# Sums of weight blocks: GpSimd additions replaced by DMAs that add into SBUF, with the seven products re-signed

## The chip, the cores and the metric

The kernel runs on one core of a Trainium2 chip. A core has five engines that each work through their own queue in order: TensorE (PE) multiplies matrices into PSUM, VectorE (DVE) and ScalarE (ACT) work on SBUF and PSUM, GpSimd (POOL) works on SBUF, and SyncE (SP) only issues DMAs. Sixteen DMA engines move data between HBM and SBUF; SP and ACT issue DMAs through hardware queues, GpSimd through a software queue. The engines wait for each other and for DMAs with semaphores. The metric is the device time of one execution in microseconds.

## The reference

The reference is one layer of a decoder trunk with 2048 rows of width 1024. All is float32. What costs time are its matrix products:

```python
u = x * (1.0 + scale[:, None, :]) + shift[:, None, :]
h = u @ w_in[l]
q, k, v, a_gate, p_in, p_gate, m_a, m_p = jnp.split(h, offsets, axis=-1)
a = sliding_window_sink_attention(q, k, v, sinks[l], bias, mask) * jax.nn.silu(a_gate)
a = a @ w_attn_proj[l]
p = jnp.einsum('bsgc,gcd->bsgd', multiscale_causal_pool(p_in), w_pool_mix[l]).reshape(B, S, POOL_WIDTH)
p = (p * pool_scale[l]) * jax.nn.silu(p_gate)
p = p @ w_pool_proj[l]
y = jax.nn.sigmoid(m_a) * a + jax.nn.sigmoid(m_p) * p
y = (y @ w_out[l]) * (1.0 + gate[:, None, :])
x = layer_norm(DEEPNORM_ALPHA * x + y, ln_gain[l], ln_bias[l])
```

`w_in` is 1024 x 6400 (16 query heads of 64, 2 key and value heads, and five widths of 1024), `w_attn_proj`, `w_pool_proj` and `w_out` are 1024 x 1024. The attention has a window of 128 with a sink for each head.

## The kernel before, in words

**Float32 by parts.** TensorE multiplies float32r operands. Each operand is split into a high part (a copy that rounds, on ScalarE, lines 312 and 319) and a low part (operand minus high part, on VectorE, through `low`, line 128). A product of blocks is then three matmuls, high by high, high by low and low by high (`mm3`).

**Seven products instead of eight.** The gates, keys and values, the attention and pool projections and the output projection are computed as 2 x 2 block products with seven block products (Winograd's form of Strassen's scheme). A `Quad` holds two weight rows; each row is 128 x 1024 and is cut in two halves of 128 x 512, so that the blocks are a11, a12 (row 0) and a21, a22 (row 1). The data side has blocks b11, b12, b21, b22, each as four tiles of 128 x 512 with high and low parts, and the sums T1 to T4 of them; these eight are the `sets`. They are made once a phase and are shared by all quads of the phase; for later phases they are written to HBM and loaded back. Before the change, with S1 = a21 + a22, S2 = S1 - a11, S3 = a11 - a21, S4 = a12 - S2 on the side of the weights and T1 = b12 - b11, T2 = b22 - T1, T3 = T2 - b11, T4 = b21 - T2 on the other, the seven are a11 b11, S1 T1, S2 T2, a12 b21, S3 T3, S4 b22 and a22 T4.

**The weight tile W.** W (`Pools.weights`, two buffers) has three places of 128 x 512. `load` (lines 270 to 277) loads a21, a22 (in a tile of its own, A22) and a11 through SP and lets GpSimd add S1 into place 1 (`sum1`, line 280). `first` gives the pair a11 and S1 to the split. `mid` (lines 282 to 286) then makes S2 and S3 in place on GpSimd (lines 284, 285) and loads a12 over a11, by a DMA that GpSimd issues. `second` gives a12 and S2, `late` (line 290) makes S4 over a12, and `third` gives S4 and S3.

**Order of one group.** Quads run in groups of two (one group has one). There are 58 quads: 17 for the gates and the keys and values in each half of the sequence, 4 for the attention projection and 4 for the pool projection in each half, and 8 for the output. In `ring`, `back` runs the second pairs of both quads (products with T2 and B21), then the third pairs (T3 and B22), then a22 (T4), and `front` runs the first pairs of the next group's quads (B11 and T1), so that a group is 14 products of twelve matmuls. Each product ends with a `tick`, at which hooks run: pieces of other work (loads and splits of sets, folding of the pool weights, sums of data blocks) that are placed by the number of the tick; `defer` puts a piece some ticks later. In `third` the next quad's `load` stands right behind the split that reads W last. The split's buffers (`w_set`, four of 128 x 1024) hold two pairs, so that a pair is split while the pair before it is multiplied. Engines keep the program's order within their queue where the code says so (`Ordered`), elsewhere a scheduler orders them.

**Stages.** The head modulates x, makes the first sets and does the sums of the first two quads on VectorE. Then come the gates of half 0, the attention of half 0, the gates of half 1, the attention of half 1 (both attentions also make the first products of the next stage, with `early_hi`, `early_lo` and `fill_one`), and last a stage of five rings: attention and pool projection of each half, and the output with the layer norm. The pool projection writes its sum to `y_d` in HBM, from which the output's quads load their weights' side.

Of the kernel before, what the change touches and what calls it, by code (L numbers as in the profile page):

```python
# [58 lines left out]
def kernel(  # L59
# [154 lines left out]
    def sums_to(ph, store, i, load, work, b12):  # L214

        b = []

        def x(r, c):
            return b[r][:, c * CH : (c + 1) * CH]

        def fetch():
            b.extend((ph.spare(), ph.spare()))
            b.reverse()
            for r in (1, 0):
                load(b[r], r)

        def sub(out, a, c):
            return lambda: pool.tensor_tensor(x(*out), x(*a), x(*c), ALU.subtract)

        todo = [(0, fetch), (3, lambda: work(b[0], 0)), (3.5, lambda: work(b[1], 1))]  # L230
        todo += [(at, sub(*z)) for at, z in (
            (7.5, ((0, 1), (0, 1), (0, 0))),
            (9, ((1, 1), (1, 1), (0, 1))),
            (10.5, ((1, 0), (1, 0), (1, 1))),
            (12, ((0, 0), (1, 1), (0, 0))),
        )]
# [25 lines left out]
    class Quad:  # L262
# [3 lines left out]

        def __init__(self, srcs, consume):
            self.srcs, self.consume = srcs, consume

        def load(self, ph, own, q=nc.sync, e=nc.gpsimd):  # L270
            self.w, self.a22 = ph.weights(), ph.last(own)
            x = self.w
            q.dma_start(x[:, 2, :], self.srcs[1][:, 0:CH])
            q.dma_start(self.a22, self.srcs[1][:, CH:])
            q.dma_start(x[:, 0, :], self.srcs[0][:, 0:CH])
            if e is not None:
                self.sum1(e)

        def sum1(self, e):
            e.tensor_tensor(self.w[:, 1, :], self.w[:, 2, :], self.a22, ALU.add)  # L280

        def mid(self, q=nc.gpsimd, e=nc.gpsimd):
            x = self.w
            e.tensor_tensor(x[:, 1, :], x[:, 1, :], x[:, 0, :], ALU.subtract)  # L284
            e.tensor_tensor(x[:, 2, :], x[:, 0, :], x[:, 2, :], ALU.subtract)  # L285
            q.dma_start(x[:, 0, :], self.srcs[0][:, CH:])

        def late(self, e=nc.gpsimd):
            x = self.w
            e.tensor_tensor(x[:, 0, :], x[:, 0, :], x[:, 1, :], ALU.subtract)  # L290

        def first(self):

            return self.w[:, 0:2]
# [5 lines left out]
        def third(self):  # L300

            return self.w[:, 0:3:2]
# [36 lines left out]
    def front(ph, q, tick):  # L339
        w = pair_split(ph, q.first())  # L340
        q.mid()
        a, b = bank(), bank()
        product(a, w[0], "B11", True)
        tick()
        product(b, w[1], "T1", True)
        tick()
        return a, b, None, None

    def back(ph, grp, opened, nxt, own, tick, b22_first=False):
        st = []  # L350
        for q, (a, b, c, w) in zip(grp, opened):
# [10 lines left out]
            nc.vector.tensor_tensor(u2, c, u2, ALU.add)  # L362
# [38 lines left out]
        for q in nxt[len(st) :]:  # L401
            q.load(ph, own)
        for q, b, c, u2, p5 in st:
# [3 lines left out]
            nc.vector.tensor_tensor(u2, c, u2, ALU.add)  # L407
# [266 lines left out]
    def attention(ph, s, q0, nxt):  # L674
# [67 lines left out]
        def finish(kind, store, m, t, src, gate):  # L742
# [7 lines left out]
            if (half, t) == (0, 1):  # L750
                pool.tensor_tensor(x, x, kept[kind, 0, 0], ALU.subtract)
# [7 lines left out]
            pool.tensor_tensor(t1, x, t1, ALU.subtract)  # L759
# [3 lines left out]
            pool.tensor_tensor(b11, t1, b11, ALU.subtract)  # L763
# [53 lines left out]

        def early_hi(x, which):
            hi, lo = ph.split(), ph.split()
            pre[x, which] = hi, lo  # L820
            act.copy(by_two(hi), nxt_group[x].first())

        def early_lo(x, which):
            hi, lo = pre[x, which]
            low(dve, by_two(lo), nxt_group[x].first(), by_two(hi))
# [3 lines left out]
        def pair(x, which):  # L829
            return halves(*pre[x, which])  # L830
# [12 lines left out]
        for n in range(N + 5):  # L843
# [221 lines left out]
    def head(ph):  # L1065
# [57 lines left out]

        def parts(name, i, src):
# [6 lines left out]
        def middle(k):  # L1131

            b1, b2 = xs[k]
            if k < 4:
                t = ts[k] = ph.p("t")
                minus(t, b2, b1)
                pool.dma_start(b12_d[k // 2, :, k % 2, :], b2)
            else:
                minus(ts[k - 4], b2, ts[k - 4])
# [5 lines left out]
        def rest_sums(i):  # L1145
            minus(xs[i][0], ts[i], xs[i][0])
# [6 lines left out]
        def products(i):  # L1153
            for w, (a, b, _, _) in zip(starts, opened):
                product(a, w[0], "B11", True, i, i + 1)
                product(b, w[1], "T1", True, i, i + 1)

        for k in range(KT):
            load(k)
            if k < 2:  # L1160
                grp[k].load(ph, False, sp, None)
# [5 lines left out]
        for k in range(2, KT):  # L1167
# [3 lines left out]
            if k == 2:  # L1171
                for q in grp:
                    q.sum1(dve)
# [15 lines left out]
        for q in grp:  # L1189
            q.late(dve)  # L1190
# [197 lines left out]
```

## Time and profile before

| what | value |
|---|---|
| time, median of 3 runs (lowest to highest) | 1850.66 us (1850.57 to 1857.23) |
| profiled execution: its time / the span of its trace | 1849.77 us / 1848.0 us |
| busy: PE / DVE / ACT / POOL | 1732.7 / 1312.4 / 942.6 / 928.6 us |
| moved by DMA | 381.32 MB, mean 206 GB/s |
| HBM read / written | 244.35 / 138.44 MB |
| granted TensorE clock, mean | 0.98 |

Busy is the time in which an engine executes; issuing a DMA, waiting on a semaphore and branches do not count. A row of a group reads: line, engine, operation, output and inputs by the program's names, count, then busy time in us and the mean of one in ns, then the engine's idle time just before the group and what ended most of it. A row of the waits reads: engine and what it was about to do, what it waited for, total us, how many times, the longest. A row of a timeline starts with the start and the length in us and has the idle time before it in brackets. L55 is the line of a helper that records many operations, so there the tile's name tells which one it is; L128 is the helper of the low parts.

### The profile page before, as it was taken

To read this page: it belongs to the slowest core of one execution; us is meant where nothing else is said; L and a number is where in the kernel's file an instruction comes from. 1 tells how busy PE (TensorE), PEld (TensorE's weight loads), DVE (VectorE), ACT (ScalarE), POOL (GpSimd) and SP (SyncE) were. 2 spreads that over 40 slices of the span, in tenths; PEclk is the share of its full clock that TensorE was granted. 3 is DMA by queue.
4 is the path that set the end of the run, shared out by engine and by line. 5 is a ranking of instruction groups with operands and counts; after the bars stand their busy time and mean duration, and the time that the engine had idled before them with its cause. 6 is when DMAs were issued, how large, how long until landed. Compare 5 with 4: busy or idle time off the path is not lost. (4 is left out here: it accounts for less than half of the span.)

```text
span 1848.0 us, 25300 instructions
## 1 busy us (share of the span) xinstructions
PE 1732.7 (94%) x8248; PEld 1437.6 (78%) x8248; DVE 1312.4 (71%) x2284; ACT 942.6 (51%) x1977; POOL 928.6 (50%) x758
## 2 busy tenths in 40 slices
PE   6789899999999999999999999999989989999996
PEld 6667677788888887787777888888867778777775
DVE  6955656554777777777766457777857887886886
ACT  4533334443777776543444367777724343422453
POOL 2234445451354667445445224456754785476553
PEclk9889999999999999999999999999999999999998
DMA  9245556677254457785776733543876574589432
GB/s 354 97 167 177 205 199 230 233 234 196 93 170 143 153 170 295 264 283 204 261 255 248 253 118 125 177 160 121 301 280 216 174 259 171 200 296 384 147 141 102
DMA packets 163571, 381.32 MB, mean 206 GB/s; under 512 B 19680, under 2 KB 23792, under 8 KB 163440
## 3 DMA queue, kind: packets, MB, share of 16 engines
q1 hardware_dynamic: 150528, 342.95, 53.3%
q0 software_dynamic: 10112, 33.06, 5.2%
q10 hardware_dynamic: 2800, 3.70, 0.9%
q8 instruction: 65, 1.06, 0.2%
q14 instruction: 66, 0.54, 0.1%
HBM read 244.35 MB, written 138.44 MB: 207 GB/s over the span
## 5 line engine op out<-in xcount | busy, mean ns | idle before, releaser
L55 PE MATMUL mm<-set_B,w_set 128*128 128x512 f32 x3240 | 809.6, 398 | 33.7 <-DVE w_set L128 23.3
L55 PEld LDWEIGHTS mm<-set_B,w_set 128*128 128x128 f32 x3240 | 606.8, 191 | 169.5 <-DVE w_set L128 32.4
L55 PE MATMUL lg<-set_T,w_set 128*128 128x512 f32 x2088 | 523.0, 400 | 49.5 <-ACT w_set L312 18.2
L55 PEld LDWEIGHTS lg<-set_T,w_set 128*128 128x128 f32 x2088 | 395.7, 192 | 152.6 <-DVE w_set L128 29.5
L128 DVE TENSOR_TENSOR w_set<-W,w_set 128x1024 fp32r<-128x1024 f32 x162 | 241.2, 1489 | 142.5 <-ACT w_set L312 137.4
L312 ACT CAST w_set<-W 128x1024 fp32r<-128x1024 f32 x162 | 169.5, 1050 | 234.6 <-PE mm L55 159.8
L55 PE MATMUL mm<-set_T,w_set 128*128 128x512 f32 x1080 | 267.1, 395 | 0.0
L55 PEld LDWEIGHTS mm<-set_T,w_set 128*128 128x128 f32 x1080 | 202.4, 190 | 42.2 <-DVE nxt L55 0.2
L284 POOL TENSOR_TENSOR W<-W 128x512 f32<-128x512 f32 x56 | 85.2, 1522 | 148.3 <-DVE w_set L128 129.0
L290 POOL TENSOR_TENSOR W<-W 128x512 f32<-128x512 f32 x56 | 80.1, 1430 | 157.8 <-DVE w_set L128 146.4
L363 POOL TENSOR_TENSOR p<-p,u 128x512 f32<-128x512 f32 x58 | 98.0, 1693 | 93.6 <-DVE u L362 91.4
L280 POOL TENSOR_TENSOR W<-W,A 128x512 f32<-128x512 f32 x56 | 82.5, 1473 | 109.1 <-DMA A<-in_win_dram 46.4
L55 DVE TENSOR_TENSOR o<-pv,o 64x128 f32<-64x128 f32 x256 | 72.4, 283 | 90.0 <-ACT o L55 87.1
L55 ACT ACTIVATE L<-L,nm 128x257 f32<-128x257 f32 (+1 forms) x256 | 127.8, 501 | 8.5 <-DVE nm L55 3.2
L55 DVE TENSOR_TENSOR k_lo<-spare,k_hi 128x512 fp32r<-128x512 f32 x88 | 89.7, 1027 | 48.4 <-ACT k_hi L55 24.4
L55 DVE CUSTOM_DVE_ANT_0 L<-lg,bt,nsink 128x256 f32<-128x256 f32 (+1 forms) x256 | 111.6, 473 | 5.3 <-PE lg L55 1.2
L285 POOL TENSOR_TENSOR W<-W 128x512 f32<-128x512 f32 x56 | 90.0, 1610 | 12.1 <-DMA W<-in_win_dram 9.5
L55 POOL TENSOR_TENSOR w_set<-W,w_set 128x1024 fp32r<-128x1024 f32 x14 | 33.7, 2408 | 122.8 <-ACT w_set L55 54.7
L55 POOL TENSOR_TENSOR p<-nxt,pg 128x512 f32<-128x512 f32 x32 | 41.4, 1294 | 105.1 <-DVE sm L55 103.8
L55 ACT COPY o<-pv 64x256 f32<-64x256 f32 x128 | 47.4, 371 | 80.8 <-PE pv L55 78.6
L55 DVE TENSOR_TENSOR ptl<-pt,pth 128x512 fp32r<-128x512 f32 (+1 forms) x128 | 85.8, 670 | 1.8 <-ACT pth L55 1.6
L55 ACT CAST k_hi<-spare 128x512 fp32r<-128x512 f32 x88 | 53.6, 616 | 55.2 <-POOL spare L55 20.3
(201 smaller groups left out, 2520.1 us busy)
## 6 DMA issues: line engine op xcount, KB each, us to landing
W<-in_win_dram SPq DMA_DIRECT2D x68, 256.0 KB, 3.8
w_set<-wmix_d SPq DMA_DIRECT2D x32, 512.0 KB, 5.4
A<-in_win_dram SPq DMA_DIRECT2D x34, 256.0 KB, 3.8
W<-in_win_dram POOLq DMA_DIRECT2D x34, 256.0 KB, 3.8
ag_d<-sig SPq DMA_DIRECT2D x32, 256.0 KB, 3.0
pg_d<-sig SPq DMA_DIRECT2D x32, 256.0 KB, 3.1
ma_d<-sig SPq DMA_DIRECT2D x32, 256.0 KB, 3.5
mp_d<-sig SPq DMA_DIRECT2D x32, 256.0 KB, 3.4
```

Of the source, the lines that this page charges most:

```text
L55: return lambda *args, **kw: self.tc.keep_in_program_order(op(*args, **kw))
L128: engine.tensor_tensor(dst, src, as32(hi), ALU.subtract)
L280: e.tensor_tensor(self.w[:, 1, :], self.w[:, 2, :], self.a22, ALU.add)
L284: e.tensor_tensor(x[:, 1, :], x[:, 1, :], x[:, 0, :], ALU.subtract)
L285: e.tensor_tensor(x[:, 2, :], x[:, 0, :], x[:, 2, :], ALU.subtract)
L290: e.tensor_tensor(x[:, 0, :], x[:, 0, :], x[:, 1, :], ALU.subtract)
L312: a.copy(by_two(hi), raw)
L363: nc.gpsimd.tensor_tensor(p5, p5, u2, ALU.add)
```

## The change

The four sums of weight blocks that GpSimd made in SBUF for each quad become DMAs issued by GpSimd with `accum_op=ALU.add`: each reads a block of the weights from HBM and adds it to what lies in its place of W. Since such a DMA only adds, the seven products are written with plus signs on the side of the weights: S1 = a21 + a22, S2' = S1 + a11, S3' = a11 + a21, S4' = S2' + a12, and on the other side T1 = b11 - b12, T2 = b22 + T1, T3 = b11 - T2, T4 = b21 - T2. The products with T1 and T2 keep their pairing, and where a product now has the other sign, the addition behind it on VectorE is a subtraction.

In W, place 0 now holds a12, place 1 the running sum and place 2 a11 and then S3'. So a12 has a place of its own and is loaded with the other blocks by SP. S1 is asked for two ticks behind the loads (`defer(2, q.sum1)`), in the attentions at step 53 where the loads are at step 51. `mid` issues two adding DMAs behind the split of the first pair, `late` one behind the split of the second. For 56 quads that is four adding DMAs in place of four GpSimd instructions and one plain DMA; a plain DMA more goes through SP. The first two quads keep their sums on VectorE, with four instructions each as before.

```diff
         def __init__(self, srcs, consume):
             self.srcs, self.consume = srcs, consume
-
-        def load(self, ph, own, q=nc.sync, e=nc.gpsimd):
+            self.a11, self.a12 = srcs[0][:, 0:CH], srcs[0][:, CH:]
+            self.a21 = srcs[1][:, 0:CH]
+
+        def load(self, ph, own, q=nc.sync, a12=True):
             self.w, self.a22 = ph.weights(), ph.last(own)
             x = self.w
-            q.dma_start(x[:, 2, :], self.srcs[1][:, 0:CH])
+            q.dma_start(x[:, 1, :], self.a21)
             q.dma_start(self.a22, self.srcs[1][:, CH:])
-            q.dma_start(x[:, 0, :], self.srcs[0][:, 0:CH])
-            if e is not None:
-                self.sum1(e)
-
-        def sum1(self, e):
-            e.tensor_tensor(self.w[:, 1, :], self.w[:, 2, :], self.a22, ALU.add)
-
-        def mid(self, q=nc.gpsimd, e=nc.gpsimd):
-            x = self.w
-            e.tensor_tensor(x[:, 1, :], x[:, 1, :], x[:, 0, :], ALU.subtract)
-            e.tensor_tensor(x[:, 2, :], x[:, 0, :], x[:, 2, :], ALU.subtract)
-            q.dma_start(x[:, 0, :], self.srcs[0][:, CH:])
-
-        def late(self, e=nc.gpsimd):
-            x = self.w
-            e.tensor_tensor(x[:, 0, :], x[:, 0, :], x[:, 1, :], ALU.subtract)
+            q.dma_start(x[:, 2, :], self.a11)
+            if a12:
+                self.load_a12(q)
+
+        def load_a12(self, q):
+            q.dma_start(self.w[:, 0, :], self.a12)
+
+        def add(self, place, src):
+            nc.gpsimd.dma_start(self.w[:, place, :], src, accum_op=ALU.add)
+
+        def sum1(self):
+            self.add(1, self.srcs[1][:, CH:])
+
+        def mid(self):
+            self.add(1, self.a11)
+            self.add(2, self.a21)
+
+        def late(self):
+            self.add(1, self.a12)
 
         def first(self):
-            return self.w[:, 0:2]
+            return self.w[:, 1:3]
 
         def second(self):
             return self.w[:, 0:2]
 
         def third(self):
-            return self.w[:, 0:3:2]
+            return self.w[:, 1:3]
...
-            nc.vector.tensor_tensor(u2, c, u2, ALU.add)
+            nc.vector.tensor_tensor(u2, u2, c, ALU.subtract)
...
+        def ask(q):
+            q.load(ph, own)
+            defer(2, q.sum1)
+
         def third(x):
             w[x] = pair_split(ph, st[x][0].third())
             if x < len(nxt):
-                nxt[x].load(ph, own)
+                ask(nxt[x])
...
-            nc.vector.tensor_tensor(p5, c, p5, ALU.add)
+            nc.vector.tensor_tensor(p5, c, p5, ALU.subtract)
...
-            if n == 51:
-                for q in nxt_group:
+            for q in nxt_group:
+                if n == 51:
                     q.load(ph, False)
+                if n == 53:
+                    q.sum1()
...
             if k in (3, 5):
-                grp[k // 2 - 1].mid(pool, dve)
+                q = grp[k // 2 - 1]
+                q.load_a12(pool)
+                plus(q.w[:, 1, :], q.w[:, 1, :], q.w[:, 2, :])
+                minus(q.w[:, 2, :], q.w[:, 1, :], q.a22)
```

The sums of data blocks (in `sums_to`, `finish` and the head) swap operands or signs in the same places, on the same engines.

More of the change, by code (lines that the diff above doesn't have):

```diff
@@ L225, in fetch, with put_sum @@
                 load(b[r], r)
-        def sub(out, a, c):
-            return lambda: pool.tensor_tensor(x(*out), x(*a), x(*c), ALU.subtract)
+        def put_sum(out, a, c, op):
+            return lambda: pool.tensor_tensor(x(*out), x(*a), x(*c), op)
         todo = [(0, fetch), (3, lambda: work(b[0], 0)), (3.5, lambda: work(b[1], 1))]
[L231 to L235, printed above, removed]
+        todo += [(at, put_sum(*z)) for at, z in (
+            (7.5, ((0, 1), (0, 0), (0, 1), ALU.subtract)),
+            (9, ((1, 1), (1, 1), (0, 1), ALU.add)),
+            (10.5, ((1, 0), (1, 0), (1, 1), ALU.subtract)),
+            (12, ((0, 0), (0, 0), (1, 1), ALU.subtract)),
         )]
@@ L401, in back @@
         for q in nxt[len(st) :]:
-            q.load(ph, own)
+            ask(q)
         for q, b, c, u2, p5 in st:
@@ L816, in attention, with raw_pair @@
         pre = {}
+        def raw_pair(x, which):
+            return nxt_group[x].second() if which else nxt_group[x].first()
         def early_hi(x, which):
@@ L820, in early_hi @@
             pre[x, which] = hi, lo
-            act.copy(by_two(hi), nxt_group[x].first())
+            act.copy(by_two(hi), raw_pair(x, which))
         def early_lo(x, which):
             hi, lo = pre[x, which]
-            low(dve, by_two(lo), nxt_group[x].first(), by_two(hi))
+            low(dve, by_two(lo), raw_pair(x, which), by_two(hi))
             if which:
```

32 lines of the change are left out of this document (17 added, 15 removed).

## The prediction

> **What bounds the kernel now.** I read the page first: the shares of the engines, the slices and the DMA queues.
>
> ```profile
> span 1848.0 us, 25300 instructions
> PE 1732.7 (94%) x8248; PEld 1437.6 (78%) x8248; DVE 1312.4 (71%) x2284; ACT 942.6 (51%) x1977; POOL 928.6 (50%) x758
> ...
> DMA  9245556677254457785776733543876574589432
> GB/s 354 97 167 177 205 199 230 233 234 196 93 170 143 153 170 295 264 283 204 261 255 248 253 118 125 177 160 121 301 280 216 174 259 171 200 296 384 147 141 102
> ...
> q1 hardware_dynamic: 150528, 342.95, 53.3%
> q0 software_dynamic: 10112, 33.06, 5.2%
> ```
>
> TensorE is busy 94% of the span, so the most that any change beside it can win is its idle time, 1848.0 - 1732.7 = 115 us. The view of windows, cut at the stages, tells where that lies (columns: window, its length, then busy time of PE, PEld, DVE, ACT and POOL, granted clock, DMA share, GB/s):
>
> ```profile
> 92.00:450.00 358.00, 330.03 (x1464) 266.80 (x1463) 211.15 (x242) 142.76 (x212) 158.04 (x133) 0.96 0.61 203
> 450.00:730.00 280.00, 277.68 (x1568) 241.99 (x1568) 207.11 (x630) 206.20 (x610) 151.67 (x125) 1.00 0.51 174
> 730.00:1030.00 300.00, 287.58 (x1234) 232.09 (x1233) 212.42 (x226) 138.23 (x211) 148.27 (x109) 0.98 0.71 252
> ...
> 1435.00:1530.00 95.00, 85.75 (x357) 68.23 (x356) 84.65 (x67) 33.93 (x40) 74.41 (x57) 0.96 0.63 216
> ...
> 1600.00:1690.00 90.00, 85.39 (x371) 68.71 (x370) 72.02 (x55) 24.37 (x30) 70.82 (x58) 1.00 0.79 288
> 1690.00:1848.00 158.00, 135.39 (x583) 109.17 (x581) 121.00 (x170) 66.91 (x103) 70.34 (x53) 0.96 0.43 160
> ```
>
> The first attention (450 to 730) leaves 2.3 us. The rings of seven products, which the change touches, leave 28.0 us in the first gates, 12.4 in the second, and 9.3, 4.6 and 22.6 in three parts of the last stage, 77 us in all. In the pool products (1435 to 1530) VectorE is busy 89% and GpSimd 78%. The waits of TensorE say for what:
>
> ```profile
> PE mm L55 <- DVE w_set L128: 23.3, 19, 3.7
> PE lg L55 <- ACT w_set L312: 18.2, 11, 5.1
> PE lg L55 <- DVE w_set L128: 15.9, 19, 5.5
> ...
> PE mm L55 <- ACT w_set L312: 6.3, 3, 2.8
> ```
>
> So 63.7 us is waiting for a weight's split: its high part (ScalarE, L312) or its low part (VectorE, L128). What follows asks what the change does to those two.
>
> **GpSimd's sums go.** Four sums for each of 56 quads (the first two quads sum on VectorE):
>
> ```profile
> L284 POOL TENSOR_TENSOR W<-W 128x512 f32<-128x512 f32 x56 | 85.2, 1522 | 148.3 <-DVE w_set L128 129.0
> L290 POOL TENSOR_TENSOR W<-W 128x512 f32<-128x512 f32 x56 | 80.1, 1430 | 157.8 <-DVE w_set L128 146.4
> L363 POOL TENSOR_TENSOR p<-p,u 128x512 f32<-128x512 f32 x58 | 98.0, 1693 | 93.6 <-DVE u L362 91.4
> L280 POOL TENSOR_TENSOR W<-W,A 128x512 f32<-128x512 f32 x56 | 82.5, 1473 | 109.1 <-DMA A<-in_win_dram 46.4
> ...
> L285 POOL TENSOR_TENSOR W<-W 128x512 f32<-128x512 f32 x56 | 90.0, 1610 | 12.1 <-DMA W<-in_win_dram 9.5
> ```
>
> and, from the same grouping for GpSimd alone, its next two groups:
>
> ```profile
> L546 POOL TENSOR_TENSOR wide<-gp,wide 128x512 f32<-128x512 f32 x32 | 50.2, 1569 | 7.6 <-DVE gp L544 7.2
> L55 POOL TENSOR_TENSOR spare<-spare 128x512 f32<-128x512 f32 x32 | 47.5, 1485 | 7.1 <-issue 4.9 <-DVE k_lo L55 1.0 <-POOL W L290 0.7
> ```
>
> That is 82.5 + 85.2 + 90.0 + 80.1 = 337.8 us of GpSimd's 928.6. GpSimd bounds nothing, so this in itself is worth 0. But it slows VectorE's splits, which have the same shape always and yet take 1.2 to 5.8 us. The instructions of the tile W (min/median/max ns, first and last start):
>
> ```profile
> L312 ACT CAST w_set<-W x162: 1029/1052/1063, 65.4 to 1817.4; 128x1024 fp32r<-128x1024 f32 x162
> L128 DVE TENSOR_TENSOR w_set<-W,w_set x162: 1205/1226/5762, 72.9 to 1818.5; 128x1024 fp32r<-128x1024 f32 x162
> ...
> L275 SPq DMA_DIRECT2D W<-in_win_dram x32: 422/426/728, 74.6 to 1014.6; - x32
> L286 POOL DMA_DIRECT2D W<-in_win_dram x32: 557/557/574, 94.2 to 1027.5; - x32
> ```
>
> The mean of those 162 is 1489 ns (row below), so they lose (1489 - 1226) x 162 = 43 us to something.
>
> ```profile
> L128 DVE TENSOR_TENSOR w_set<-W,w_set 128x1024 fp32r<-128x1024 f32 x162 | 241.2, 1489 | 142.5 <-ACT w_set L312 137.4
> ```
>
> The longest lies beside GpSimd additions that follow each other without a gap, of which these are two (timeline, VectorE and GpSimd):
>
> ```profile
> 1653.18 5.76 DVE L128 TENSOR_TENSOR w_set<-W,w_set 128x1024 fp32r<-128x1024 f32 x1 [0.23 <-ACT w_set L312]
> ```
>
> ```profile
> 1654.07 1.29 POOL L280 TENSOR_TENSOR W<-W,A 128x512 f32<-128x512 f32 x1
> ...
> 1656.57 1.28 POOL L285 TENSOR_TENSOR W<-W 128x512 f32<-128x512 f32 x1
> ```
>
> In the rings GpSimd's other long work is L363 and the two groups of 50.2 and 47.5, so the removed sums are 337.8 of 533.5 us, 63%. Of TensorE's 39.2 us behind L128 some 6 are the half microsecond that any late high part brings after it; of the other 33, 63% is 21 us as one end, and 0 the other, if VectorE was late through the length of its queue alone. I take two thirds of 21, **-14 us**, since the longest waits lie in the stages where both engines are fullest. A long wait also costs clock: ten matmuls took 4.14 us after a wait of 3.73 us, and 2.56 after 1.57.
>
> ```profile
> 1503.85 4.14 PE L55 MATMUL mm<-set_B,w_set 128*128 128x512 f32 x10 [3.73 <-DVE w_set L128]
> ...
> 1512.73 2.56 PE L55 MATMUL mm<-set_B,w_set 128*128 128x512 f32 x10 [1.57 <-DVE w_set L128]
> ```
>
> Two such fewer are **-3 us** (0 to -9).
>
> **The block a12 is loaded early, by SP.** Before, GpSimd sent for it after L284, because it took the place of a11. ScalarE waited for it and for GpSimd's sums:
>
> ```profile
> ACT sig L517 <- DMA wmix_d<-st_lo: 27.8, 3, 9.8
> ...
> ACT w_set L312 <- DMA W<-in_win_dram: 16.4, 4, 6.0
> ...
> ACT w_set L312 <- POOL W L280: 11.4, 4, 4.0
> ```
>
> Those two are 27.8 us of ScalarE. TensorE's whole waiting for the high part is 18.2 + 6.3 = 24.5 us, and part of it follows other waits in ScalarE's queue, such as the one for a store above them. **-4 us**, ends 0 and -24.5. The 56 more issues on SP, at 0.43 us, are 24 us in a queue that is not the bound; behind them stand stores whose buffers ScalarE reuses, cost 0 unless the queue backs up (counted with the DMA load below).
>
> **Four accumulating DMAs for each quad.** The trace has none, so the cost is bounded. On GpSimd's queue an issue takes 557 to 574 ns (row above): 224 issues less 56 that go to SP, 168 x 0.56 = 94 us, which leaves GpSimd at about 685 us; hidden. The wait that matters is from issue to landing. GpSimd's plain transfers of this size, and all loads into this tile (min/median/max):
>
> ```profile
> DMA to landing us min/median/max: 2.8/3.7/6.3
> ```
>
> ```profile
> DMA to landing us min/median/max: 2.5/3.7/12.9
> ```
>
> So the ends are 2.8 and 12.9 us. I take 5: the median and something for the destination that has to be read too. What it is hidden under: a product of twelve matmuls takes 2.72 us.
>
> ```profile
> 174.81 2.88 PE L55 MATMUL mm<-set_B,w_set 128*128 128x512 f32 x12
> 177.53 2.93 PE L55 MATMUL lg<-set_T,w_set 128*128 128x512 f32 x12
> ```
>
> A group is 14 products, 38 us. The four split buffers let a quad's first, second and third split start four products apart, 10.9 us; less 1.05 + 1.23 = 2.3 us for the split itself, 8.6 us are left for the sum between them. Before, the second split's a12 took 1.5 + 0.56 + 3.7 = 5.8 us of that and the third's sum 1.4. After, both take 0.56 + 5. So 0, with 3 us to spare, and about 112 x each microsecond over it as an upper end; the two quads of a group are late together, so 56 x is what I would count. The first sum is asked for two products after its loads and has about six products; 0. A late one stands in front of GpSimd's L363 add and the later adds of the other quad, as the sums did.
>
> The DMA engines: 33.06 MB took 5.2% of 1848 us, so 256 KB take 0.76 us of all sixteen. 224 more are 170 us, share 59.6 to 69%. Stores and loads that ScalarE and VectorE wait for land later by perhaps 15%; on the 24.5 - 4 us of TensorE's waits for ScalarE that is **+3**. Where the queue is full already, 1600 to 1690 with 0.79, sixteen adds are 12 us of 90 and the next stage's sets and rows come later: **+5** (0 to +15).
>
> The Trainium skill, Collectives: The Full Stack, section The bandwidth ceiling, says that the add in the DMA path costs little in itself but needs two source reads, so that its rate is half a copy's. No run here shows it yet; by that page the 170 us would be 340. The trace's price for a copy is the one that the sum uses.
>
> The Trainium skill, SBUF — State Buffer, section SBUF: two separate sides, warns against moving work to DMAs issued by GpSimd, since a VectorE instruction that holds both ports keeps it from writing descriptors. The 32 issues above lie within 17 ns of each other beside a VectorE that is busy 71%, so the trace does not agree for the instructions of this kernel; by that page each add would be late by up to the length of one VectorE instruction, still under the 3 us spare.
>
> **Signs and order.** The products trade adds for subtractions on the same engines with the same shapes, the places in the weight tile change, and the head does its eight sums on VectorE as before: 0. Only a12 of the head arrives earlier, which nothing waits for.
>
> **Sum.** Against the profiled execution of 1849.8 us (0.9 below the median of 1850.7): -14 - 3 - 4 + 3 + 5 = -13, so 1836.8; on the median's scale **1837 us**.
>
> **Rivals.**
> - Slower: the accumulating DMA lands after more than 8.0 us (8.6 less the issue). Then each second and third split is late, 28 groups x 2 x the excess. At 9 us that is +56, and 1837 + 56 = 1893; at 8.4 it is +22 and 1859. For it: the maximum of 12.9, stages with DMA shares of 0.71 and 0.79. Against: a median of 3.7. It decides from about 8.2 us.
> - No change: each add takes the DMA engines 1.5 us instead of 0.76, for the second read. Then sixteen in the window from 1600 are 24 of 90 us on a share of 0.79, which is full; the rings from 730 get 0.71 + 0.30. I add 6 + 4 us there and 3 more for ScalarE's waits: 1837 + 13 = 1850. Against it: a share of 0.71 at 252 GB/s is not the limit, since another slice moves 384. (The doubled rate is that of the Trainium skill, Collectives: The Full Stack, as above.)
> - Much faster: VectorE's and GpSimd's mutual delay is what all ring waits come from. Half of the 77 us gone is 1850.7 - 38 = 1812. For it: the 89% of VectorE at 1435. Against: 24.5 us of waits are ScalarE's, and the end of the last window is the last rows' own.
>
> **How the numbers follow.** A measurement of this kernel tells about 0.5%, 9.3 us, from no change: 1841.4 to 1859.9. Forecast (1820 to 1841) 0.33, much faster 0.14, no change 0.17, slower 0.36, of which I put 0.14 beyond 1890. The forecast's own range is 1820 to 1848. With 0.05 below 1802 the range 1802 to 1890 leaves out 0.19. Faster 0.47, same 0.17, slower 0.36.
>
> **What the profile after would show.** L128's mean falls from 1489 towards 1300 ns and TensorE's waits for it below 30 us; GpSimd near 685 us; the accumulating DMAs land in 4 to 6 us; no wait of ScalarE's L312 split for a W transfer totals over 20 us. The prediction is wrong if they land in 8 us or more, if ScalarE's waits for W grow past 100 us, or if L128's mean stays while the sums are gone.

## The result and the profile after

The changed kernel takes 1899.99 us (median of 4 runs, 1895.87 to 1904.26), the kernel before beside it 1850.62 us: ratio 1.0268 with the interval 1.0245 to 1.0291, **49 us slower**. The prediction said 1837 and a range up to 1890. The profiled execution has a span of 1902.2 us, 54.2 more than before. From the page after, the shares of the engines, the slices of the DMA share and the queues:

```profile
span 1902.2 us, 25529 instructions
PE 1748.9 (92%) x8248; PEld 1442.0 (76%) x8248; DVE 1226.1 (64%) x2284; ACT 940.1 (49%) x1977; POOL 748.2 (39%) x702
...
DMA  9378798986344579899989833555988898899864
...
q1 hardware_dynamic: 158592, 357.64, 54.0%
q0 software_dynamic: 37888, 77.11, 20.8%
```

VectorE (1312.4 to 1226.1) and GpSimd (928.6 to 748.2) have less work, and still TensorE is idle 153.3 us, 38 more than before, and busy 16 us more with the same matmuls. The software queue grew from 5.2% to 20.8% of the sixteen engines, and outside the attentions the slices of the DMA share are mostly at 8 and 9, where they were at 5 to 7. The same windows as before (columns as there):

```profile
92.00:450.00 358.00, 327.32 (x1453) 263.00 (x1453) 201.83 (x241) 143.11 (x213) 117.36 (x120) 0.97 0.86 243
450.00:730.00 280.00, 278.92 (x1577) 243.16 (x1575) 207.53 (x630) 204.31 (x609) 146.47 (x122) 1.00 0.55 180
730.00:1030.00 300.00, 271.44 (x1121) 217.52 (x1122) 173.96 (x210) 124.84 (x191) 91.47 (x86) 0.95 0.91 274
```

The DMA share in the gates went from 0.61 to 0.86 and from 0.71 to 0.91; in the second gates TensorE does 1121 matmuls in 300 us where it did 1234, and its granted clock falls from 0.98 to 0.95. The attention between them hardly changes. The waits of TensorE, then of ScalarE, for what the change touches:

```profile
PE mm L55 <- DVE w_set L128: 38.1, 28, 4.8
PE lg L55 <- ACT w_set L318: 23.6, 13, 6.7
PE lg L55 <- DVE w_set L128: 16.9, 22, 5.5
PE lg L55 <- DMA set_T<-u_T_split: 9.7, 2, 6.2
PE lg L55 <- DMA set_T<-ain_T_split: 9.1, 3, 6.7
...
PE mm L55 <- ACT w_set L318: 6.1, 3, 4.4
```

```profile
ACT w_set L318 <- DMA W<-y_d: 52.3, 10, 11.0
ACT w_set L318 <- DMA W<-in_win_dram: 45.9, 12, 7.5
ACT w_set L318 <- DMA W<-in_wpp_dram: 16.8, 4, 5.7
ACT w_set L318 <- DMA W<-in_wap_dram: 13.9, 2, 10.2
```

The waits for splits are 84.7 us (63.7 before), and behind them ScalarE waits 128.9 us for transfers into W, in 28 waits. Which transfers these are is told by the view of line 286, which before issued the plain DMA of a12 and now issues the adds. Who waited for it, and for how many us and how often, before and after:

```profile
ACT w_set L312: 37.3, 10
```

```profile
ACT w_set L318: 128.8, 28
```

So all 28 waits end with an adding DMA, none with a plain load. Two groups, and the instructions of lines 128 and 286 (min/median/max ns), the last line being the landing of the adding DMAs of L286 in us:

```profile
L128 DVE TENSOR_TENSOR w_set<-W,w_set 128x1024 fp32r<-128x1024 f32 x162 | 218.1, 1347 | 177.3 <-ACT w_set L318 173.6
...
L286 POOL DMA_DIRECT2D W<-in_win_dram x128 | 112.2, 950 | 408.8 <-DVE w_set L128 238.0
```

```profile
L128 DVE TENSOR_TENSOR w_set<-W,w_set x162: 1207/1225/3705, 73.0 to 1872.8; 128x1024 fp32r<-128x1024 f32 x162
L286 POOL DMA_DIRECT2D W<-in_win_dram x128: 850/874/1219, 77.5 to 1068.1; - x128
```

```profile
DMA to landing us min/median/max: 3.6/6.2/11.5
```

VectorE's splits did become faster (mean 1489 to 1347 ns). An adding DMA takes GpSimd 0.95 us to issue, not 0.56, and lands after 6.2 us; counted from the trace, 31 of the 224 take 8 us or more. They aren't alone in being late: the plain transfers of the same size, before, after, and in the changed kernel with its adds left out (first experiment; count, KB each, median us to landing):

```profile
W<-in_win_dram SPq DMA_DIRECT2D x68, 256.0 KB, 3.8
...
A<-in_win_dram SPq DMA_DIRECT2D x34, 256.0 KB, 3.8
...
ag_d<-sig SPq DMA_DIRECT2D x32, 256.0 KB, 3.0
```

```profile
W<-in_win_dram SPq DMA_DIRECT2D x100, 256.0 KB, 5.4
...
A<-in_win_dram SPq DMA_DIRECT2D x34, 256.0 KB, 6.2
ag_d<-sig SPq DMA_DIRECT2D x32, 256.0 KB, 4.5
```

```profile
W<-in_win_dram SPq DMA_DIRECT2D x100, 256.0 KB, 4.6
...
A<-in_win_dram SPq DMA_DIRECT2D x34, 256.0 KB, 4.7
ag_d<-sig SPq DMA_DIRECT2D x32, 256.0 KB, 4.1
```

So a part of this lateness, 0.8, 0.9 and 1.1 us, is there without any add, in the new form itself (its 100 loads by SP hold a12 besides a21 and a11); the adds bring 0.8, 1.5 and 0.4 us more.

Where the time went by stage shows in the first and last start of the loads into W. The last load of the gates and the loads of the output projection, before, after, and with the adds left out:

```profile
L273 SPq DMA_DIRECT2D W<-in_win_dram x32: 327/333/609, 74.2 to 1014.2; - x32
...
L273 SPq DMA_DIRECT2D W<-y_d x8: 319/327/870, 1649.4 to 1780.3; - x8
```

```profile
L276 SPq DMA_DIRECT2D W<-in_win_dram x32: 327/332/543, 74.3 to 1043.5; - x32
...
L276 SPq DMA_DIRECT2D W<-y_d x8: 319/326/542, 1699.2 to 1835.3; - x8
```

```profile
L276 SPq DMA_DIRECT2D W<-in_win_dram x32: 327/332/688, 73.5 to 980.9; - x32
...
L276 SPq DMA_DIRECT2D W<-y_d x8: 319/327/417, 1606.0 to 1733.8; - x8
```

Against the form without adds, the changed kernel is 63 us behind at the end of the gates, 93 at the start of the output and 102 at its end. Both the gates and the last rings lose.

### The profile page after: what moved, and what is told of

It is laid out like the page before. It is cut to its first block, busy times and chain, and to the rows that moved or that the text cites. A ratio compares the mean times of both kernels' runs of the same rounds, so it can differ in the third digit from the quotient of the medians.

```text
span 1902.2 us, 25529 instructions
## 1 busy us (share of the span) xinstructions
PE 1748.9 (92%) x8248; PEld 1442.0 (76%) x8248; DVE 1226.1 (64%) x2284; ACT 940.1 (49%) x1977; POOL 748.2 (39%) x702
## 3 DMA queue, kind: packets, MB, share of 16 engines
q0 software_dynamic: 37888, 77.11, 20.8%
## 5 line engine op out<-in xcount | busy, mean ns | idle before, releaser
L55 PE MATMUL mm<-set_B,w_set 128*128 128x512 f32 x3240 | 813.4, 399 | 50.9 <-DVE w_set L128 38.1
L55 PE MATMUL lg<-set_T,w_set 128*128 128x512 f32 x2088 | 534.2, 406 | 70.9 <-ACT w_set L318 23.6
L55 PEld LDWEIGHTS lg<-set_T,w_set 128*128 128x128 f32 x2088 | 400.5, 195 | 180.8 <-DVE w_set L128 31.2
L128 DVE TENSOR_TENSOR w_set<-W,w_set 128x1024 fp32r<-128x1024 f32 x162 | 218.1, 1347 | 177.3 <-ACT w_set L318 173.6
L286 POOL DMA_DIRECT2D W<-in_win_dram x128 | 112.2, 950 | 408.8 <-DVE w_set L128 238.0
L369 POOL TENSOR_TENSOR p<-p,u 128x512 f32<-128x512 f32 x58 | 91.7, 1589 | 122.3 <-DVE u L368 113.0
L55 DVE TENSOR_TENSOR k_lo<-spare,k_hi 128x512 fp32r<-128x512 f32 x88 | 74.0, 846 | 95.1 <-ACT k_hi L55 44.3
L55 PE MATMUL lg<-kk,qs 128*128 128x256 f32 (+1 forms) x512 | 80.5, 279 | 0.0
L55 ACT CAST pth<-pt 128x512 fp32r<-128x512 f32 (+1 forms) x128 | 73.5, 574 | 10.6
L55 ACT ACTIVATE L<-L,sm 128x256 f32<-128x256 f32 (+1 forms) x128 | 64.3, 502 | 26.8 <-DVE sm L55 26.7
```

The costliest lines, as they stand in the source:

```text
L55: return lambda *args, **kw: self.tc.keep_in_program_order(op(*args, **kw))
L128: engine.tensor_tensor(dst, src, as32(hi), ALU.subtract)
L286: nc.gpsimd.dma_start(self.w[:, place, :], src, accum_op=ALU.add)
L369: nc.gpsimd.tensor_tensor(p5, p5, u2, ALU.add)
```

## The experiments

Two theories. **Load**: an adding DMA takes the sixteen DMA engines about 1.5 us instead of 0.76, so that all transfers land later. **Chain**: the adds' own issue and landing are too late for the split that waits for them. They don't exclude each other, since by the first the adds land later too. Differences below are the ratio's, times 1850.66 us; the intervals are 3 to 7 us to each side.

**1. No adds.** `add` does nothing.

```diff
-            nc.gpsimd.dma_start(self.w[:, place, :], src, accum_op=ALU.add)
+            pass
```

> The changed kernel with the 224 adding DMAs left out: W holds a12, a21 and a11 as loaded and is split so (the weights' sums are not made, so the output is another one). Two theories on the 49 us. LOAD: each adding DMA takes the sixteen DMA engines some 1.5 us (q0 rose from 5.2% to 20.8%), and every other transfer lands later, on which ScalarE, VectorE and GpSimd wait. CHAIN: the adds themselves land too late for the next split (median 6.2 us behind an issue of 0.95 us, in a gap of 8.6 us), the load on others matters little. Both expect here the change without its price: the gain of 13 to 21 us that was forecast for GpSimd's removed work and the early a12, so about 1830 to 1837 us. If it is above 1845, the gain itself was not there, and the forecast failed on that side too.

1803.4 us, ratio 0.9746 (0.9715 to 0.9776), -47 us. So the adds cost 97 us, and what the change takes away is worth far more than I had put on it (experiments 9 to 11).

**2. Plain DMAs in place of the adding ones.** Same instructions in the same order, without the addition.

```diff
-            nc.gpsimd.dma_start(self.w[:, place, :], src, accum_op=ALU.add)
+            nc.gpsimd.dma_start(self.w[:, place, :], src)
```

> The changed kernel with each adding DMA made a plain one of the same blocks (it overwrites the place, so the sums are not made and the output is another one): the same number of instructions in the same order, the same dependences. LOAD expects each to take about 0.76 us of the DMA engines in place of 1.5, so half of the added load, and a time about half-way between the kernel without adds and the change: 1860 to 1870 us. CHAIN expects a landing of 4 to 5 us, which fits the gap, and so 1832 to 1845 us.

1855.5 us, ratio 1.0015 (0.9995 to 1.0034). The plain copies cost 50 us and the adding 47 more. That is 4.5 us under the range of the load theory and 10.5 over that of the chain theory.

**3. Adds of 64 of the 512 columns.** Every issue and wait stays.

```diff
-            nc.gpsimd.dma_start(self.w[:, place, :], src, accum_op=ALU.add)
+            nc.gpsimd.dma_start(self.w[:, place, 0:64], src[:, 0:64], accum_op=ALU.add)
```

> The changed kernel with each adding DMA cut to 64 of the 512 columns (the sums are made in those columns only, so the output is another one): the same 224 issues with the same dependences and nearly the same order, an eighth of the bytes. Without adds the kernel took 1803.4 us, with plain ones 1855.5, with adding ones 1900. LOAD, by its time on the DMA engines (0.2 us each in place of 1.5): 1803 + 97/8 = 1815 us, 1808 to 1822. CHAIN, in which the issue and the fixed part of the landing count (an issue near 0.9 us and a landing of some 3 us, each in a chain): half of the price or more stays, 1835 to 1860 us.

1822.04 us, ratio 0.9836 (0.9808 to 0.9863): the upper end of what load had expected. An issue still takes 0.95 us on GpSimd, so the issue time costs at most the 17 us that are left. The software queue of the three, each with its span:

```profile
span 1800.8 us, 24928 instructions
...
q0 software_dynamic: 5632, 18.38, 2.8%
```

```profile
span 1856.2 us, 25529 instructions
...
q0 software_dynamic: 23552, 77.11, 12.4%
```

```profile
span 1818.4 us, 25565 instructions
...
q0 software_dynamic: 37888, 25.73, 7.4%
```

Share times span, less the 50.4 us that the queue has without adds (0.028 x 1800.8), over 224: a plain copy takes the sixteen engines (0.124 x 1856.2 - 50.4) / 224 = 0.80 us, an adding one (0.208 x 1902.2 - 50.4) / 224 = 1.54 us, and one of 64 columns 0.38 us.

**4 and 5. One add less.** Without the DMA that makes S3', which has the most time, or without the one that makes S2', which the second split waits for.

```diff
             self.add(1, self.a11)
-            self.add(2, self.a21)
```

> The changed kernel without the add that makes S3' (a11 stays in its place; the output is another one). It stands in no tight place: its result is wanted only by the third split. LOAD: a quarter of the load, so a quarter of the 97 us: 1872 to 1880 us. CHAIN: nearly nothing, 1892 to 1900, since the adds that the splits wait for are all still there.

```diff
-            self.add(1, self.a11)
             self.add(2, self.a21)
```

> The changed kernel without the add that makes S2', for which the second split waits (the place keeps S1; the output is another one). The same engines' order as the kernel without the add of S3', and the same load. LOAD expects the same time as that one, 1872 to 1880 us. CHAIN expects much less, 1835 to 1865, since the second split then waits for nothing that GpSimd issues behind the first split.

1867.64 us (ratio 1.0092, 1.0057 to 1.0128) and 1865.79 us (1.0066, 1.0043 to 1.0089), 4 and 6 us below what load had expected, and equal within their intervals. If a late sum alone were the cause, the hurried one would have been worth more. Against the form without adds, with ScalarE's waits that end with one of these DMAs (who waited for line 286, as above):

| kernel | DMA engines' time for the adds | ScalarE's waits for them | cost over no adds |
|---|---|---|---|
| adds of 64 columns | 84 us | 27.1 us | 17 us |
| plain copies | 180 us | 59.0 us | 50 us |
| no S3' / no S2' | 265 / 271 us | 120.9 / 89.4 us | 64 / 59 us |
| changed kernel | 345 us | 128.8 us | 97 us |

The cost follows the DMA engines' time at 0.2 to 0.28 us for each, whatever makes it: plain, adding, hurried or not. The splits' waits for these DMAs grow with it, so this table doesn't part load from chain. Only the two kernels with one add less speak against the waits as the measure: their load and cost are nearly the same, and their waits differ by 31 us.

**6 and 7. The load on the kernel before.** Behind each of GpSimd's sums goes a DMA that adds the same block into memory that nothing reads; then the same with 64 columns.

```diff
+        def spill(self, src):
+            k = spilled[0] = (spilled[0] + 1) % SCR
+            pool.dma_start(scr[k], src, accum_op=ALU.add)
...
+                self.spill(self.srcs[1][:, CH:])
```

> The kernel before, with the load alone added: behind each of its 224 sums on GpSimd one adding DMA of the same block, into one of four blocks of HBM in turn that nothing reads. Nothing of the products waits for them. LOAD expects a time near or above the change, 1880 to 1910 us, with all landings later as in the change. CHAIN expects 1850 to 1862, what 224 more issues on GpSimd's queue may cost.

1984.26 us, ratio 1.0715 (1.0676 to 1.0754): +132, more than load alone had allowed.

```diff
-            pool.dma_start(scr[k], src, accum_op=ALU.add)
+            pool.dma_start(scr[k][:, 0:64], src[:, 0:64], accum_op=ALU.add)
```

> This is the kernel before with a DMA that adds behind each of GpSimd's sums, as in the loaded kernel before, but each adds 64 of the 512 columns into memory that nothing reads: the output is whole. It keeps the 224 issues on GpSimd's queue (0.95 us each, 213 us in all) and takes seven eighths of the bytes away. If the +134 us of the loaded kernel were transfers on the DMA engines, the time is 1860 to 1885 us: an eighth of the price, and something for sums that start an issue later. If they were the issues in GpSimd's queue, it stays at 1950 to 1985 us.

1912.34 us, ratio 1.0354 (1.032 to 1.0387): +66, between the two expectations. The issues alone cost here, because GpSimd also makes its sums: 128 of the 224 in the view of groups are

```profile
L55 POOL DMA_DIRECT2D scr<-in_win_dram x128 | 115.0, 977 | 1.3 <-issue 1.1
```

an instruction of about a microsecond in front of the next sum. If the small transfers cost the 17 us here that they cost in experiment 3, some 49 of the 66 are issue time in a busy queue, and 132 - 49 = 83 the load of the whole ones. No run tests this division, and experiment 8 shows that a target in memory has a price of its own.

**8. The load without the wait.** The changed form without sums; the 224 adds go to memory that nobody waits for.

```diff
-            nc.gpsimd.dma_start(self.w[:, place, :], src, accum_op=ALU.add)
+            k = spilled[0] = (spilled[0] + 1) % SCR
+            pool.dma_start(scr[k], src, accum_op=ALU.add)
```

> This is the changed kernel with the 224 adds aimed at memory that nothing reads and nobody waits for; the sums of weights are not made, so the product is not the reference's. Issues and bytes stay, the wait of ScalarE and TensorE for the adds is gone. Load theory (each add takes 1.5 us or more of the sixteen DMA engines and every other transfer lands later): 1880 to 1930 us, as the changed kernel. Chain theory (the adds' own landing is what the splits wait for): 1803 to 1830 us, as without any adds.

1971.12 us, ratio 1.0674 (1.0645 to 1.0703). So the load costs without the chain: no split waits for an add, and it is slower still. That doesn't show that the splits' waits for adds cost nothing in the changed kernel, since this run is slower than load had it too and has waits of its own. The adds take the engines 1.6 us each here, and GpSimd waits for earlier ones:

```profile
L55 POOL DMA_DIRECT2D scr<-in_win_dram x128 | 108.5, 1033 | 71.3 <-DMA scr<-in_win_dram 71.3
```

Why a target in memory costs that much more than one in SBUF wasn't settled.

**9. GpSimd's sums in the new form.**

```diff
-            self.add(1, self.a11)
-            self.add(2, self.a21)
+            x = self.w
+            nc.gpsimd.tensor_tensor(x[:, 1, :], x[:, 1, :], x[:, 2, :], ALU.add)
+            nc.gpsimd.tensor_tensor(x[:, 2, :], x[:, 1, :], self.a22, ALU.subtract)
...
```

> The changed kernel's re-signed products, its layout of W and its early a12, but the four sums are made by GpSimd instructions again (S3' as S2' minus a22). The forecast's term for the early a12 was -4 us (0 to -24.5), and signs and order 0: 1846 us, with 1826 to 1851 as ends. LOAD and CHAIN both expect it below the changed kernel by about 50 us, and GpSimd near 920 us busy again. If it is near 1900, the cause is in the layout, the loads through SP or the deferred first sum, and both theories fall.

1863.08 us, ratio 1.0071 (1.0045 to 1.0097), above the ends of the expectation: the new form with the old engine is 13 us slower than the kernel before. So something in the new form beside the adds costs time; experiments 10 and 11 look for it.

**10. The kernel before without GpSimd's sums.** a21 goes to place 1, and the third pair is places 0 and 1.

```diff
-            q.dma_start(x[:, 2, :], self.srcs[1][:, 0:CH])
+            self.whole = e is None
+            q.dma_start(x[:, 2 if self.whole else 1, :], self.srcs[1][:, 0:CH])
...
-            if e is not None:
-                self.sum1(e)
...
+            if self.whole:
+                e.tensor_tensor(x[:, 1, :], x[:, 1, :], x[:, 0, :], ALU.subtract)
...
```

> This is the kernel before without GpSimd's 224 sums of weights: a21 is loaded to the place of the first sum, the products use the blocks as they are, and the block a12 is still sent for by GpSimd once the first split has been made; the product is not the reference's. It is to say what the changed form's 1803 us without adds is owed to. If the sums are what costs in the kernel before (through VectorE's splits and the wait for the sums themselves), it is 1803 to 1815 us. If the early a12 and the new places are worth as much as the sums, it stays at 1825 to 1840 us, as the prediction's first term (14 to 21 us for the sums) would have it.

1792.48 us, ratio 0.9684 (0.9655 to 0.9712): below the expected range. GpSimd's sums hold 58 us, and the old form without sums is 11 us faster than the new one without sums. Its shares and TensorE's first waits:

```profile
span 1784.4 us, 25030 instructions
PE 1706.5 (96%) x8248; PEld 1429.8 (80%) x8248; DVE 1207.6 (68%) x2284; ACT 941.5 (53%) x1977; POOL 591.7 (33%) x534
```

```profile
PE mm L55 <- DVE w_set L128: 10.0, 10, 2.5
PE lg L55 <- DVE w_set L128: 8.8, 8, 5.5
...
PE lg L55 <- ACT w_set L314: 7.6, 6, 3.5
```

The span is 63.6 us shorter than before (this execution ran 6 us under the median of its kernel): 37.4 of it idle time and 26.2 TensorE's busy time, with the mean granted clock at 0.989 instead of 0.980 (0.972 in the changed kernel).

**11. When a12 is loaded.** Both runs are without sums: `add` does nothing, as in experiment 1. First GpSimd sends for it where `mid` stands; then it also goes to the place of a11, so that it has to wait for the first split.

```diff
-        def load(self, ph, own, q=nc.sync, a12=True):
+        def load(self, ph, own, q=nc.sync, a12=False):
...
         def mid(self):
+            self.load_a12(nc.gpsimd)
```

> This is the changed kernel's form without any sums, but the block a12 is sent for by GpSimd at the place in its queue where the sums between the splits stood, as in the kernel before, and not by SP with the other loads; the product is not the reference's. The changed form without sums took 1803 us, the kernel before without sums 1792. If the early load by SP is what makes the changed form slower (four blocks at once in one queue), it is 1788 to 1797 us; if the places in the weight tile or the re-signed products do, it is 1800 to 1806 us.

1805.91 us, ratio 0.9742 (0.9723 to 0.976), as with SP. But GpSimd had nothing to wait for and sent for a12 in the same microseconds as SP for the other blocks, so this told only that the queue doesn't matter.

```diff
-            q.dma_start(self.w[:, 0, :], self.a12)
+            q.dma_start(self.w[:, 2 if self.ring else 0, :], self.a12)
...
-            return self.w[:, 0:2]
+            return self.w[:, 1:3] if self.ring else self.w[:, 0:2]
```

> This is the changed form without sums, with the block a12 loaded by GpSimd into the place of a11, so that it must wait for the first split, as in the kernel before; the order of the instructions on TensorE, ScalarE, GpSimd and SP is that of the kernel before without sums, and VectorE differs by the signs alone; the product is not the reference's. In the run before this one GpSimd sent for a12 in the same 2 us as SP for the other blocks, so it left the four loads together. If four blocks asked for at once are what makes the changed form slower than the one before (1803 against 1792 us without sums), it is 1788 to 1797 us; if the signs or the places are, 1800 to 1808 us.

1795.15 us, ratio 0.9688 (0.9655 to 0.972), that of the old form (0.9684). So four blocks asked for at once cost about 10 us. The same 68 loads that SP makes for W, in the first of these two runs, with a12 beside them, and in the second:

```profile
W<-in_win_dram SPq DMA_DIRECT2D x68, 256.0 KB, 4.6
```

```profile
W<-in_win_dram SPq DMA_DIRECT2D x68, 256.0 KB, 3.9
```

**12. Other engines for the sums.** Half by DMA (S1, S3') and half by GpSimd; all four on VectorE; S2' and S4' on VectorE with S1 and S3' on GpSimd; and the kernel before with S2 and S4 (L284, L290) on VectorE. The last one's edit:

```diff
-            e.tensor_tensor(x[:, 1, :], x[:, 1, :], x[:, 0, :], ALU.subtract)
+            nc.vector.tensor_tensor(x[:, 1, :], x[:, 1, :], x[:, 0, :], ALU.subtract)
...
-            e.tensor_tensor(x[:, 0, :], x[:, 0, :], x[:, 1, :], ALU.subtract)
+            nc.vector.tensor_tensor(x[:, 0, :], x[:, 0, :], x[:, 1, :], ALU.subtract)
```

> The changed kernel with S1 and S3' made by adding DMAs and S2' and S4', for which a split waits soonest, by GpSimd instructions. Both resources have half of the work: 112 adds (LOAD: 48 us over 1803.4) and 112 GpSimd sums (half of what all four cost in the same form, (1863.1 - 1803.4)/2 = 30 us). If the prices add, 1882 us; if a price grows faster than the work, since a half-loaded queue hides more, below 1850, which would beat both kernels. CHAIN expects the second, 1835 to 1850.

> This is the changed kernel's form with all four sums of weights made by VectorE in place of the DMAs, S3' as S2' less a22; the output is whole. No DMA load, and GpSimd has no sum to make. VectorE gets 224 sums of 0.69 us by its own rows of 512 columns, 154 us, and was busy 1226 of 1902 us. Load theory: without the adds the form runs in 1803 us, and what comes on top is only what VectorE's splits come later by; the chain per set is longer by four times 0.69 us on VectorE, so 1815 to 1850 us, at or under the kernel before. Chain theory (any serial sum in the slot is dear): 1850 to 1880 us.

> This is the changed kernel's form with S2' and S4' made by VectorE and S1 and S3' by GpSimd (S3' as S2' less a22); the output is whole. No DMA load; GpSimd's half of the sums is 169 us, VectorE gets 112 of 0.69 us, 77 us. Load theory: 1815 to 1850 us, between the form without sums and that with GpSimd's sums (1863 us). If only GpSimd's slow sums cost, half of the 60 us they cost goes: 1833 us.

> This is the kernel before with the two sums that stand between splits, L284 and L290, made by VectorE (0.7 to 0.9 us each in its earlier runs) instead of GpSimd (1.4 to 1.5 us), and the other two left on GpSimd; the output is whole. If a sum costs by how long the split waits for it and by GpSimd's running beside VectorE's splits, as in the new form with two sums on each, the time is 1825 to 1842 us. If the new form's 1843 us came from the early a12, it is 1845 to 1860 us here.

| sums made by | time | ratio (interval) |
|---|---|---|
| DMA and GpSimd | 1879.94 us | 1.015 (1.0117 to 1.0183) |
| VectorE | 1845.65 us | 0.9986 (0.9971 to 1.0002) |
| VectorE and GpSimd, new form | 1843.03 us | 0.9965 (0.9948 to 0.9982) |
| VectorE and GpSimd, old form | 1842.88 us | 0.9953 (0.9935 to 0.9971) |

The mix costs 75 us over no sums, where half of the DMAs' 97 and half of GpSimd's 60 are 78: the prices add. The last two beat the kernel before by some 6 to 9 us. On whatever engine, the four sums cost 40 to 60 us over the same form without them; the DMAs' 97 is the dearest.

## Why the prediction was wrong

**What was right.** GpSimd's sums did slow VectorE's splits: the mean fell from 1489 to 1347 ns and the longest from 5762 to 3705, and with the sums back on GpSimd in the new form (experiment 9) the mean is 1498. The form without adds is 47 us faster, so there was a gain to be had. Of the three marks that I set for a wrong prediction, one came: ScalarE's waits for W passed 100 us. TensorE's waits for L128 are 38.1 + 16.9 = 55.0 us, not below 30, because its splits now start later.

**The step that failed: the adds at 0, with +3 and +5 for the DMA load.** I took the price of a plain copy, 0.76 us of the sixteen engines, and called a share of 0.61 or 0.71 room enough. An add takes 1.54 us, and the room isn't free: each microsecond of added DMA time cost 0.2 to 0.28 us of the kernel (experiments 1 to 5), long before the share reaches 1. The 345 us cost 97, and even plain copies, 180 us at nearly the price that I had taken, cost 50 and not 8. The sums weren't hidden either. I had 5 us for the landing and 3 to spare; the median is 6.2, and all 28 waits of ScalarE for transfers into W, 128.8 us, end with an add. Only 5 of these 28 adds took 8 us or more, the others landed in 4.0 to 7.9 us: the 8 us that I had allowed were not free. Other transfers land later too, by 0.4 to 1.5 us against the form without adds. Had the add cost what a copy does, the kernel would have been at the time of before (experiment 2).

The Trainium skill, Collectives: The Full Stack, section The bandwidth ceiling, has the add of a ring's reduce step need two source reads and run at half a copy's rate; 1.54 against 0.80 us agrees. The Trainium skill, DMA: Bandwidth & Descriptors, section SWDGE vs HWDGE vs iDMA, says that a DMA engine takes turns between the queues that software and hardware feed. That SP's loads into W land 0.8 us later with the adds in GpSimd's queue than without them (5.4 and 4.6 us) agrees with it; no run here shows the turns themselves.

**The rivals.** "No change" had the right mechanism, 1.5 us for each add, and priced it at 13 us. It counted only the stage whose queue was full and 7 us elsewhere; the loads into W show the loss in the gates as in the last rings. "Slower" had nearly the right time, 1893, and a part of the mechanism: adds do land too late for splits. But it priced a landing of 9 us for every second and third sum, which wasn't reached (median 6.2), and nothing for the load: removing the hurried add was worth no more than the other, and without any split that waits for an add the time still rose (experiment 8). That its sum came near is luck in part. What stays open is how much of the 97 us comes by the adds' own later landing (4.1 us with 64 columns, 6.2 whole), which the splits' waits show, and how much by the other transfers.

**The gain, mis-sized: -14 for VectorE's splits and -3 for the clock.** The sums held 58 us (experiment 10), where my ends for these two terms together allowed 21 + 9. I had let only TensorE's waits for L128 go, and only 63% of them. Without sums all waits for splits fall, from 63.7 to 26.4 us and what other waits followed them, and TensorE's busy time falls by 26 us: I had bounded that second part at 9 from two long waits. In the changed kernel the same part works against it, +16 us busy at a clock of 0.972: (1 - 0.972) x 1902.2 is 53 us of clock not granted, where (1 - 0.980) x 1848.0 is 37, a difference of 16. That the two agree isn't a rule: without sums the same working gives 17 us for the 26, so the clock is a part of it and the rest stays open.

**The early a12: -4 predicted, +10 measured** (experiment 11, without sums). I asked which waits it would remove, and not what four blocks in flight at once do to each other. The waits themselves I had read short: ScalarE waited 37.3 us for GpSimd's DMA of a12, of which the row that I took has 16.4.

**Smaller sizes.** GpSimd at 748 us, not 685: the issue takes 0.95 us, not 0.56. In the changed kernel that costs at most 17 us (experiment 3); in a queue that also makes sums some 49 us, by the untested division in experiment 7. Landing 6.2 us, not 5. And one bound was misread: an add held back for one VectorE instruction wouldn't have stayed under the 3 us spare, since the longest that I had shown took 5.76; the adds' issues, 845 to 1574 ns, show no hold of that length.

Together: what the change takes away was worth -47 where I had -14 - 3 - 4 = -21, and what it adds cost +97 where I had +8. The direction turned on the second.

## What to carry to other kernels

Price a DMA that adds as two copies on the DMA engines, and look at what else waits for those engines: here a share of 0.6 to 0.7 left no free room, and each microsecond of added DMA time cost about a quarter of a microsecond. Before replacing work, measure the kernel without it: the form without sums says in one run what there is to win (58 us), and which engine makes the sums most cheaply is then a matter of four more. A load that can go early isn't free if it lands among others that are needed first.

## What was not expected of the hardware

- A DMA that adds takes GpSimd 0.95 us to issue in the mean (median 0.87) where a plain one takes 0.55, and 0.95 also when it moves an eighth of the bytes.
- An adding DMA of 64 columns (256 bytes in each partition's row) takes the engines 0.38 us, a quarter of the whole one's 1.54, not an eighth.
- The same adds aimed at memory instead of SBUF cost 172 us over no adds instead of 97, with no split waiting for them; GpSimd waited 71.3 us for earlier ones.
- TensorE's busy time moved by 42 us between the kernel before without sums and the changed one (1706.5 to 1748.9), and to 1775.1 in experiment 6, with the same matmuls, so what these forms lose is not idle time alone. The granted clock goes the same way in the first two (0.989 and 0.972), but not everywhere: experiment 8 has 0.952 with 1762.2 us busy, experiment 6 0.962.
